# Between two layers: tile 1's last residual update and some weight splits set behind tile 0's first products, and buffers of their own for what meets there

## The chip, the cores and the metric

The kernel runs on one core of a Trainium2 chip. Its engines are named as in the profile: PE multiplies matrices, DVE and ACT do elementwise work, POOL and SP stand beside them, and SP issues the loads. Each engine has its own queue of instructions and runs it in order; semaphores let one wait for another. The metric is the device time of one execution in microseconds, as the median of several runs.

## The reference

A decoder trunk of two layers on 256 tokens of width 2048, batch 1, all in float32. Layer 0 mixes tokens with RWKV-7, layer 1 with latent attention (MLA) on a key and value store that is computed once from the residual stream. Each layer ends in a squared-ReLU MLP of width 8192. Every sub-layer is normed on both sides and gated:

```python
h = rms_norm(x, norm_g[l, 0]) * (1.0 + scale_m) + shift_m
y = rwkv7_time_mix(h, ...)  # layer 0;  mla_attention(h, ...) in layer 1
x = x + gate_m * rms_norm(y, norm_g[l, 1])
h = rms_norm(x, norm_g[l, 2]) * (1.0 + scale_f) + shift_f
y = squared_relu_mlp(h, mlp_up[l], mlp_down[l])
x = x + gate_f * rms_norm(y, norm_g[l, 3])
# between the layers, from the x that layer 0 leaves:
hs = rms_norm(x, kv_in_g)
ckr = hs @ kv_down
```

`scale_*`, `shift_*` and `gate_*` come from one conditioning vector `c` by `silu(c) @ ada_w[l] + ada_b[l]`.

## The kernel before

The 256 tokens are two token tiles of 128 (`t` is 0 or 1). The residual stream `xr` stays on the chip, tokens on partitions, 2048 values a row. Products need channels on partitions, so at the start of a sub-layer the normed residual is turned by PE and scaled (`affine4`).

Weights come from memory in units of 128x2048 float32, 1 MB, loaded by SP into a buffer `raw`. A unit is split in two halves of 128x1024 (`unit`, `hilo`): ACT casts the half to the high part `whi` (L172) and DVE subtracts to get the low part `wlo` (L173). Each product is then three matmuls (`mm3`: high x high, low x high, high x low; L218 to L220). The pool `split` holds `WB_MLP` or `WB_MLA` pairs of such halves. Where that pool is not to be used, `unit` is given other room (`spare`, `spare_part`), and the halves are then named `spare`.

The change is about three seams, where one sub-layer's last products have to become the next one's input:

1. RWKV's output projection (`proj_tail`, products `po`) to the MLP of layer 0 (`begin`, products `pup`)
2. the down products of that MLP (`pd`) to the shared latent (`kvd`, products `pl`)
3. the attention's output projection (`po`) to the MLP of layer 1 (`pup`)

At each seam the class `Residual` finishes the old sub-layer. `block(t, n, ...)` takes a block of 512 columns: it adds what lies there already, squares it on ACT for the norm (`square_sum`, written to `junk`) and multiplies it with the gate row `G`. `update(t)` takes the norm factor `rs` of tile `t` (`rstd`, a reduction `rrv` and seven small DVE steps, L151 to L168) and adds the two halves of 1024 columns to `xr` (L976), ACT squares the result for the next norm. `last` does the last block and `update` for tile 0 and for tile 1 and returns the next norm's factors `rx0` and `rx1` together.

The new sub-layer then scales the identity with tile `t`'s factor (`dg`, L1114 or L1327), and PE multiplies `xr` by it in 16 transposes a tile (`trt`, L1030), four to a group `g`. `affine4` brings a group to the input: four steps `hc`, taken in turn by DVE and ACT, a cast on ACT and a subtraction on DVE (to `h`, or `o1h` and `o1l` in seam 2). `products(t, g)` are 12 matmuls, four rows of channels times three. The order on PE is written out by hand (`manual_schedule`): 16 transposes of tile 0, (0,0), (0,1), 16 transposes of tile 1, (1,0), (1,1), (0,2), (0,3), (1,2), (1,3). On the other engines a scheduler sets the order when the program is built; `issue_after(x)` holds what is written under it back until `x` has been issued. Units 0 and 1 of the new weight go to the split pool, and units 2 and 3 to spare room, issued after tile 1's `dg`.

Of the kernel before, what the change touches and what calls it, by code (L numbers as in the profile page):

```python
# [12 lines left out]
F32 = mybir.dt.float32  # L13
F32R = mybir.dt.float32r
# [62 lines left out]
def trunk_kernel(ctx: ExitStack, tc: tile.TileContext, a, out, dbg=None):  # L77
# [93 lines left out]
    def hilo(hi, lo, x):  # L171
        ACT.copy(hi, x)  # L172
        return DVE.tensor_sub(lo, x, hi.bitcast(F32))  # L173

# [213 lines left out]
    with ExitStack() as s0:  # L388
# [3 lines left out]
        p1 = pool(s0, "p1", 1)  # L392

        XS = []
        xs0 = p1.tile([P, 4, 4, T], F32R, tag="xs0", name="xs")
# [4 lines left out]
        with ExitStack() as s1:  # L400
# [10 lines left out]
            def spot():  # L411
# [60 lines left out]
            for cb in range(4):  # L472
# [9 lines left out]
                XS.append(p1.tile([P, 4, 4, T], F32R, tag=f"xs{cb}", name="xs") if cb else xs0)  # L482
# [68 lines left out]
        with ExitStack() as s2:  # L551
# [361 lines left out]
            while nxt < KT or flying:  # L913
                if nxt < KT and len(flying) < LONG and steps >= STAGGER * nxt:
# [29 lines left out]
        with ExitStack() as s3:  # L944
# [5 lines left out]
            G0 = p1.tile([P, KT, T], F32R, tag="xs3", name="G0").bitcast(F32).rearrange("p k c -> p (k c)")  # L950
# [3 lines left out]
            class Residual:  # L954
# [16 lines left out]
                def update(self, t, then=None):  # L971
                    rs = rstd(self.ss, t, D, "rn")
# [60 lines left out]
    def affine4(t, g, ps, sc, bi, hi, lo, tp):  # L1033

        q, ks = slice(t * P, (t + 1) * P), slice(g * 4, g * 4 + 4)
        h = tp.tile([P, 4, P], F32, tag="hc", name="hc", bufs=2)
# [9 lines left out]
        hilo(hi[:, ks, q], lo[:, ks, q], h)  # L1046

    def to_channels(xn, sc, bi, hi, lo, tp, tags=("rw",), kts=range(KT)):

        for kt in kts:  # L1050
# [4 lines left out]
            h = tp.tile([P, 2, T], F32, tag="hc", name="hc", bufs=2)[:, 0, :]  # L1055
# [14 lines left out]

    def mlp(l, x, rx, ada_rate, aside=None):
        with ExitStack() as s:
            psum(s, rw=5, pj=3)

            mh = pool(s, f"mlc{l}", 1)
            m2 = pool(s, f"mlq{l}", 2)
            mp = pool(s, f"mlp{l}", 1)
            ya = mp.tile([P, 2, D], F32, name="ya")
            split["more"] = pool(s, "more", MORE_MLP)
# [23 lines left out]
            def begin():  # L1103

                A = mod_scale(l, 4, 2)
                parts = [p_ for k in range(2) for p_ in unit(a["up0"][l, k])]
# [4 lines left out]
                def turn(t, gs):  # L1111
                    if 0 in gs:
                        dg[t] = mh.tile([P, P], F32, tag="dg", name="dg", bufs=2)
                        turned.append(DVE.tensor_scalar(dg[t], ident, rx[t], None, ALU.mult).ins)  # L1114
                    for g in gs:
                        trs[t, g] = transposes(x[:, t, :], dg[t], g)

                def products(t, g):
# [3 lines left out]
                dg, turned = {}, []  # L1122
                with tc.manual_schedule(engines={mybir.EngineType.PE}):
                    for t in range(2):
                        turn(t, range(4))
                        for g in range(4):
                            affine4(t, g, trs[t, g], A, mods[l, 3], hh, hl, mh)
                            if g < 2:
                                products(t, g)
                    with tc.issue_after(turned[1]):  # L1130
                        for k in (2, 3):
                            parts += unit(a["up0"][l, k], room=spare)
                    for t in range(2):
                        for g in (2, 3):
                            products(t, g)
                for t in range(2):
                    u = mh.tile([P, 512], F32, tag="hc", name="u0", bufs=2)
# [108 lines left out]
    with ExitStack() as s4:  # L1246
# [5 lines left out]
        ckcq = qa.tile([P, 4, 4, T], F32R, tag="ckcq", name="ckcq")  # L1252
        ckT, cqT = [ckcq[:, z] for z in range(2)], [ckcq[:, 2 + z] for z in range(2)]
        qs = pool(s4, "qs", 1)
        qv = pool(s4, "qv", 1)
        q2 = pool(s4, "q2", 1)
# [20 lines left out]
        if True:  # L1277
# [4 lines left out]
            def latent(pss, gname, dst):  # L1282
# [6 lines left out]
                for j in range(4):  # L1289
# [3 lines left out]
                    h = q2.tile([P, 2, T], F32, tag="hc", name="hc", bufs=2)[:, 0, :]  # L1293
# [27 lines left out]
            parts = [p_ for k in range(2) for p_ in unit(a["kvd"][k])]  # L1321
            trs, dg, turned = {}, {}, []

            def turn(t, gs):
                if 0 in gs:
                    dg[t] = q2.tile([P, P], F32, tag="dg", name="dg", bufs=2)
                    turned.append(DVE.tensor_scalar(dg[t], ident, rx[t], None, ALU.mult).ins)  # L1327
                for g in gs:
# [243 lines left out]
```

## Time and profile before

| | us |
|---|---|
| runs | 2584.51, 2598.10, 2595.97 |
| median | 2595.97 |
| profiled execution | 2599.04 |
| its span | 2597.3 |
| PE busy in the span | 2487.8 |
| DVE busy | 1945.7 |
| ACT busy | 1312.5 |

The times inside the profile are counted from the start of the span, which is 1.7 us shorter than the time of that execution. In rows of the order in time, the columns are start, duration, engine, line, operation, what it writes and reads, the shapes and how many were merged; in square brackets stands how long the engine had been idle before it, and who ended the wait. A matmul row's duration overlaps the next one's, so distances between starts tell how fast products follow. The granted clock was 0.98 of full speed over the span.

### The profile page before, as it was taken

To read this page: it belongs to the slowest core of one execution; us is meant where nothing else is said; L and a number is where in the kernel's file an instruction comes from. 1 tells how busy PE (TensorE), PEld (TensorE's weight loads), DVE (VectorE), ACT (ScalarE), POOL (GpSimd) and SP (SyncE) were. 2 spreads that over 40 slices of the span, in tenths; PEclk is the share of its full clock that TensorE was granted. 3 is DMA by queue.
4 is the path that set the end of the run, shared out by engine and by line. 5 is a ranking of instruction groups with operands and counts; after the bars stand their busy time and mean duration, and the time that the engine had idled before them with its cause. 6 is when DMAs were issued, how large, how long until landed. Compare 5 with 4: busy or idle time off the path is not lost.

```text
span 2597.3 us, 39264 instructions
## 1 busy us (share of the span) xinstructions
PE 2487.8 (96%) x15048; PEld 2060.5 (79%) x15048; DVE 1945.7 (75%) x3823; ACT 1312.5 (51%) x2361; POOL 70.9 (3%) x150
## 2 busy tenths in 40 slices
PE   6998999999997999999999999999899999999998
PEld 3667887888776888888888878778788888888886
DVE  4787887888877788888888867776676665555555
ACT  3555675766646444444444456544544444444443
POOL 0000110111100000000000000000000000000000
PEclk8899998999998999999999999999999999999999
DMA  9755544455575688888888824657567555555553
GB/s 374 293 192 196 178 173 153 166 180 186 171 265 205 227 331 327 331 322 328 327 332 332 328 103 156 217 176 254 210 223 260 186 190 195 189 185 194 192 184 127
DMA packets 87885, 594.54 MB, mean 229 GB/s; under 512 B 10128, under 2 KB 14480, under 8 KB 16784
## 3 DMA queue, kind: packets, MB, share of 16 engines
q1 hardware_dynamic: 87696, 592.03, 63.0%
q8 instruction: 118, 1.93, 0.3%
q14 instruction: 71, 0.58, 0.1%
HBM read 589.89 MB, written 2.10 MB: 228 GB/s over the span
## 4 chain that ended last, share of the span: by engine, by line
PE 77%; DVE 8%; ACT 4%; issue 1%; DMA 1%; POOL 0%; DVEq 0%; ACTq 0%
PE pup L233 17%; PE pd L218 9%; PE pd L220 9%; PE pd L219 9%; PE pup L234 9%; DVE wlo L173 2%; DVE raw L320 1%; PE po L219 1%; PE po L220 1%; PE po L218 1%; PE rk L223 1%; PE rk L224 1%; PE rk L225 1%; PE pl L218 1%; PE ar L720 1%
## 5 line engine op out<-in xcount | busy, mean ns | idle before, releaser
L172 ACT CAST whi<-raw 128x1024 fp32r<-128x1024 f32 x729 | 743.9, 1023 | 895.1 <-PE pd L220 355.9
L173 DVE TENSOR_TENSOR wlo<-raw,whi 128x1024 fp32r<-128x1024 f32 x729 | 864.0, 1188 | 439.0 <-ACT whi L172 436.1
L233 PE MATMUL pup<-h,whi 128*128 128x512 f32 x1920 | 677.8, 398 | 0.0
L234 PE MATMUL pup<-h,wlo 128*128 128x256 f32 x1920 | 539.2, 281 | 0.0
L233 PEld LDWEIGHTS pup<-h,whi 128*128 128x128 f32 x1920 | 360.6, 188 | 88.5
L218 PE MATMUL pd<-whi,uh 128*128 128x512 f32 x1024 | 399.0, 390 | 0.0
L220 PE MATMUL pd<-whi,ul 128*128 128x512 f32 x1024 | 398.6, 389 | 0.0
L320 DVE SCALAR_TENSOR_TENSOR raw<-raw,crow 128x1024 f32<-128x1024 f32 x320 | 389.4, 1225 | 12.0 <-DMA raw<-in_adat_dram 12.0
L219 PE MATMUL pd<-wlo,uh 128*128 128x512 f32 x1024 | 398.4, 389 | 0.0
L234 PEld LDWEIGHTS pup<-h,wlo 128*128 128x128 f32 x1920 | 362.7, 189 | 0.5
L220 PEld LDWEIGHTS pd<-whi,ul 128*128 128x128 f32 x1024 | 192.2, 188 | 40.4
L218 PEld LDWEIGHTS pd<-whi,uh 128*128 128x128 f32 x1024 | 192.2, 188 | 40.0
L219 PEld LDWEIGHTS pd<-wlo,uh 128*128 128x128 f32 x1024 | 192.2, 188 | 39.5
L223 PE MATMUL rk<-xs,whi 128*128 128x256 f32 x512 | 155.5, 304 | 2.9 <-ACT rS L595 2.2
L225 PE MATMUL rk<-xs,wlo 128*128 128x256 f32 x512 | 150.1, 293 | 2.1 <-DVE wlo L173 2.0
L224 PE MATMUL rk<-xs,whi 128*128 128x256 f32 x512 | 148.6, 290 | 0.0
L223 PEld LDWEIGHTS rk<-xs,whi 128*128 128x128 f32 x512 | 98.7, 193 | 9.3 <-ACT rS L595 4.1
L225 PEld LDWEIGHTS rk<-xs,wlo 128*128 128x128 f32 x512 | 98.8, 193 | 4.5 <-DVE wlo L173 3.0
L224 PEld LDWEIGHTS rk<-xs,whi 128*128 128x128 f32 x512 | 98.7, 193 | 1.8
L732 DVE TENSOR_TENSOR xt<-ar,X 128x60 f32<-128x60 f32 (+14 forms) x240 | 49.3, 206 | 22.3 <-ACT ar L721 20.0
L1188 DVE TENSOR_TENSOR ya<-pd,ya 128x512 f32<-128x512 f32 x96 | 61.5, 682 | 0.0
L219 PE MATMUL pv<-wlo,xsv 128*128 128x512 f32 x128 | 55.1, 431 | 5.0 <-DVE wlo L173 4.8
(431 smaller groups left out, 3620.5 us busy)
## 6 DMA issues: line engine op xcount, KB each, us to landing
raw<-in_adat_dram SPq DMA_DIRECT2D x160, 1024.0 KB, 6.9
raw<-in_up_dram SPq DMA_DIRECT2D x128, 1024.0 KB, 4.9
raw<-in_dn_dram SPq DMA_DIRECT2D x128, 1024.0 KB, 4.9
early<-in_ada_dram SPq DMA_DIRECT2D x17, 1024.0 KB, 11.9
raw<-in_wr_dram SPq DMA_DIRECT2D x16, 1024.0 KB, 5.0
raw<-in_wk_dram SPq DMA_DIRECT2D x16, 1024.0 KB, 5.9
raw<-in_wo_dram SPq DMA_DIRECT2D x16, 1024.0 KB, 5.2
raw<-in_mo_dram SPq DMA_DIRECT2D x16, 1024.0 KB, 5.3
```

What stands on the lines that cost most here:

```text
L172: ACT.copy(hi, x)
L173: return DVE.tensor_sub(lo, x, hi.bitcast(F32))
L218: PE.matmul(ps, lh, rh, start=start, stop=False)
L219: PE.matmul(ps, lh, rl, start=False, stop=False)
L220: PE.matmul(ps, ll, rh, start=False, stop=stop)
L223: PE.matmul(ps, wh, xh, start=start, stop=False)
L224: PE.matmul(ps, wh, xl, start=False, stop=False)
L225: PE.matmul(ps, wl, xh, start=False, stop=stop)
L233: PE.matmul(ps, hi[:, s], x2[:, kt].rearrange("p e t -> p (e t)"), start=(kt == 0), stop=False)
L234: PE.matmul(ps[:, T:], lo[:, s], x2[:, kt, 0, :], start=False, stop=(kt == KT - 1))
L320: DVE.scalar_tensor_tensor(raw[:, s], raw[:, s], 1.0, crow[:, s], ALU.mult, ALU.mult, accum_out=part[:, kt, half : half + 1])
L1188: DVE.tensor_add(y, pss[t], y)
```

## The change

`last` now returns tile 0's factor and a function `later`, which does tile 1's update and its factor when it is called. Both seams' code goes through one new function, `tiles_first`. It splits five halves of the new weight (units 0 and 1 and the first half of unit 2) into the split pool, which holds five pairs now, and turns tile 0. After affine (0,1) it issues the second half of unit 2 into spare room, `later` and affine (0,2). The products of (0,2) come before tile 1's transposes. The split of unit 3 and affine (0,3) are issued after affine (1,1). In the attention layer the scalings `xn` of the residual come after affine (1,3).

Buffers: `hc` and `dg` move to a pool `seam` that lives through the whole program. The four blocks `xs` of the RWKV layer become four pools. `ckcq` gets a pool of its own, the pool `more` of raw units is opened ahead of the MLP's `ya`, `EARLY` goes from 3 to 4, and the build gives the scratch room of dynamic loads 8192 bytes.

```diff
-WB_MLP = 4
-WB_MLA = 4
+WB_MLP = 5
+WB_MLA = 5
...
-EARLY = 3
+EARLY = 4
...
+    def split_part(raw, at, room=None):
+        if room:
+            hi, lo = room()
+        else:
+            hi = split["hi"].tile([P, 1024], F32R, tag="whi", name="whi")
+            lo = split["lo"].tile([P, 1024], F32R, tag="wlo", name="wlo")
+        hilo(hi, lo, raw[:, at * 1024 : at * 1024 + 1024])
+        return hi, lo
...
+    seam = pool(ctx, "seam", 1)
...
                     self.block(0, n, pss[0], more)
                     self.update(0)
+                    rs0 = rstd(self.xs, 0, D, "rx0")
                     self.block(1, n, pss[1], more)
-                    rs = [rstd(self.xs, 0, D, "rx0")]
-                    self.update(1)
-                    rs.append(rstd(self.xs, 1, D, "rx1"))
-                    return rs
+                    rs1 = rstd(self.ss, 1, D, "rn")
+
+                    def later():
+                        self.update(1, rs=rs1)
+                        return rstd(self.xs, 1, D, "rx1")
+
+                    return rs0, later
...
+    def tiles_first(rx, units, room, turn, affine, products):
+        rs0, later = rx
+        parts = [p_ for src in units[:2] for p_ in unit(src)]
+        raw = load(units[2])
+        parts.append(split_part(raw, 0))
+
+        def wait(*ins):
+            for i_ in ins:
+                held.enter_context(tc.issue_after(i_))
+
+        with tc.manual_schedule(engines={mybir.EngineType.PE}):
+            turn(0, rs0)
+            for g in range(2):
+                ready = affine(0, g)
+                products(parts, 0, g)
+            with ExitStack() as held:
+                wait(*ready)
+                parts.append(split_part(raw, 1, room))
+                rs1 = later()
+                affine(0, 2)
+            products(parts, 0, 2)
+            turn(1, rs1)
+            for g in range(2):
+                ready = affine(1, g)
+                products(parts, 1, g)
+            with ExitStack() as held:
+                wait(*ready)
+                parts.extend(unit(units[3], room=room))
+                affine(0, 3)
+            products(parts, 0, 3)
+            for g in (2, 3):
+                ready = affine(1, g)
+                products(parts, 1, g)
+        return ready
...
-            for t in range(2):
-                for n in range(2):
-                    s = slice(n * 1024, (n + 1) * 1024)
-                    DVE.tensor_scalar(xn[:, t, s], x[:, t, s], rx[t], None, ALU.mult)
+            ready = tiles_first(rx, [a["kvd"][k] for k in range(4)], spare_part, turn, affine, products)
+            with tc.issue_after(ready[1]):
                 for t in range(2):
+                    for n in range(2):
+                        s = slice(n * 1024, (n + 1) * 1024)
+                        DVE.tensor_scalar(xn[:, t, s], x[:, t, s], rxs[t], None, ALU.mult)
...
-    nc = bacc.Bacc("TRN2", target_bir_lowering=False, num_devices=1)
+    nc = bacc.Bacc("TRN2", target_bir_lowering=False, num_devices=1, dynamic_dma_scratch_size=8192)
```

What this does to the order on the engines is seen at three places. The number after L is the line of the kernel that is listed, so L976 and L989, or L1327 and L1370, are the same statement before and after.

On DVE at seam 2, from update(0) (`xr`) to tile 0's `dg`, before the change (`ya` is the MLP's sum, `rrv` to `rsu` are steps of the norm):

```order
L976 SCALAR_TENSOR_TENSOR xr<-ya,rsy,xr 128x1024 x2
L967 TENSOR_TENSOR ya<-pd_15940,ya 128x512
L376 TENSOR_REDUCE rrv<-ssx 128x1
L151 TENSOR_SCALAR rsy<-rrv 128x1
L157 SCALAR_TENSOR_TENSOR rst<-rsy,rrv 128x1
L163 SCALAR_TENSOR_TENSOR rsy<-rst,rsy 128x1
L157 SCALAR_TENSOR_TENSOR rst<-rsy,rrv 128x1
L166 TENSOR_SCALAR rsu<-rst 128x1
L167 TENSOR_TENSOR rsu<-rsu,rst 128x1
L168 SCALAR_TENSOR_TENSOR rsy<-rsu,rsy 128x1
L1327 TENSOR_SCALAR dg<-ident,rsy 128x128
```

After the change, the last twelve rows of the same stretch:

```order
L166 TENSOR_SCALAR rsu<-rst 128x1
L982 TENSOR_TENSOR ya<-ya,G 128x512
L167 TENSOR_TENSOR rsu<-rsu,rst 128x1
L389 TENSOR_REDUCE rrv<-ss 128x1
L173 TENSOR_TENSOR wlo<-raw,whi 128x1024
L168 SCALAR_TENSOR_TENSOR rsy<-rsu,rsy 128x1
L151 TENSOR_SCALAR rsy<-rrv 128x1
L173 TENSOR_TENSOR wlo<-raw,whi 128x1024
L157 SCALAR_TENSOR_TENSOR rst<-rsy,rrv 128x1
L173 TENSOR_TENSOR wlo<-raw,whi 128x1024
L163 SCALAR_TENSOR_TENSOR rsy<-rst,rsy 128x1
L1370 TENSOR_SCALAR dg<-ident,rsy 128x128
```

Two more rows `wlo` stand between these and update(0): all five halves are now split there, where none was, and steps of tile 1's norm have come in among them.

On ACT at the same place, the squares of the old blocks and of `xr`, and the casts among them, before the change:

```order
L386 ACTIVATE junk,ss<-ya 128x512 x3
L386 ACTIVATE junk,ssx<-xr 128x1024
L172 CAST spare<-raw 128x1024
L386 ACTIVATE junk,ssx<-xr 128x1024
L172 CAST spare<-raw 128x1024
L386 ACTIVATE junk,ss<-ya 128x512
L172 CAST spare<-raw 128x1024 x2
L386 ACTIVATE junk,ssx<-xr 128x1024 x2
L1043 ACTIVATE hc<-trt,pcol 128x128 x3
```

And after:

```order
L399 ACTIVATE junk,ss<-ya 128x512 x3
L399 ACTIVATE junk,ssx<-xr 128x1024
L172 CAST whi<-raw 128x1024
L399 ACTIVATE junk,ssx<-xr 128x1024
L172 CAST whi<-raw 128x1024
L399 ACTIVATE junk,ss<-ya 128x512
L172 CAST whi<-raw 128x1024 x3
L1061 ACTIVATE hc<-trt,pcol 128x128 x2
```

The casts of the first five halves stand where those of units 2 and 3 stood, and the squares of tile 1's `xr` have gone behind the first `hc`.

On DVE at seam 3, the end of tile 1's update and tile 0's `dg`, before the change:

```order
L167 TENSOR_TENSOR rsu<-rsu,rst 128x1
L168 SCALAR_TENSOR_TENSOR rsy<-rsu,rsy 128x1
L976 SCALAR_TENSOR_TENSOR xr<-yG_18116,rsy,xr 128x1024 x2
L1114 TENSOR_SCALAR dg<-ident,rsy 128x128
L376 TENSOR_REDUCE rrv<-ssx 128x1
```

After, from `dg` to the first step of affine (0,2):

```order
L1167 TENSOR_SCALAR dg<-ident,rsy 128x128
L166 TENSOR_SCALAR rsu<-rst 128x1
L167 TENSOR_TENSOR rsu<-rsu,rst 128x1
L168 SCALAR_TENSOR_TENSOR rsy<-rsu,rsy 128x1
L1059 TENSOR_SCALAR hc<-trt,A_18856,mod_92 128x128 x3
L1065 TENSOR_TENSOR h_18855<-hc,h_18855 128x4x128
L1059 TENSOR_SCALAR hc<-trt,A_18856,mod_92 128x128
L1065 TENSOR_TENSOR h_18855<-hc,h_18855 128x4x128
L989 SCALAR_TENSOR_TENSOR xr<-yG_18133,rsy,xr 128x1024
L173 TENSOR_TENSOR spare<-raw,spare 128x1024
L989 SCALAR_TENSOR_TENSOR xr<-yG_18133,rsy,xr 128x1024
L1059 TENSOR_SCALAR hc<-trt,A_18856,mod_92 128x128
```

Tile 1's update (`xr`) has gone from ahead of `dg` to behind affine (0,1), with half a spare split between its halves. Ahead of this `dg`, five rows `wlo` stand among the norm steps as in seam 2, and in seam 1 one `wlo` stands ahead of update(0) and the add of tile 1's block ahead of the multiply of tile 0's.

More of the change, by code (lines that the diff above doesn't have):

```diff
@@ L391, in trunk_kernel @@
         splits(s0, WB)
-        p1 = pool(s0, "p1", 1)
+        p1 = [pool(s0, f"p1{j}", 1) for j in range(4)]
         XS = []
-        xs0 = p1.tile([P, 4, 4, T], F32R, tag="xs0", name="xs")
+        xs0 = p1[0].tile([P, 4, 4, T], F32R, tag="xs0", name="xs")
         def xs_at(w, z, kt):
@@ L1045, in affine4, with to_channels @@
                 ACT.activation(h[:, j, :], ps[:, o], AF.Identity, scale=s, bias=b)
-        hilo(hi[:, ks, q], lo[:, ks, q], h)
-    def to_channels(xn, sc, bi, hi, lo, tp, tags=("rw",), kts=range(KT)):
+        cast = ACT.copy(hi[:, ks, q], h).ins
+        return cast, DVE.tensor_sub(lo[:, ks, q], h, hi[:, ks, q].bitcast(F32)).ins
+    def to_channels(xn, sc, bi, hi, lo, tags=("rw",), kts=range(KT)):
         for kt in kts:
@@ L1109, in begin, with turn, affine, products @@
                 trs = {}
[L1111 to L1118, printed above, removed]
+                def turn(t, rs):
+                    dg = seam.tile([P, P], F32, tag="dg", name="dg", bufs=2)
+                    DVE.tensor_scalar(dg, ident, rs, None, ALU.mult)
+                    for g in range(4):
+                        trs[t, g] = transposes(x[:, t, :], dg, g)
+                def affine(t, g):
+                    return affine4(t, g, trs[t, g], A, mods[l, 3], hh, hl)
+                def products(parts, t, g):
                     for kt in range(4 * g, 4 * g + 4):
                         part_products(pss[t], t, kt, (*parts[kt // 2], kt % 2), hh, hl, kt == 0, kt == KT - 1)
-                dg, turned = {}, []
-                with tc.manual_schedule(engines={mybir.EngineType.PE}):
-                    for t in range(2):
[L1125 to L1135, printed above, removed]
+                tiles_first(rx, [a["up0"][l, k] for k in range(4)], spare, turn, affine, products)
                 for t in range(2):
-                    u = mh.tile([P, 512], F32, tag="hc", name="u0", bufs=2)
+                    u = seam.tile([P, 512], F32, tag="hc", name="u0", bufs=2)
                     ACT.activation(u, pss[t], AF.Relu)
@@ L1319, in spare_part @@
                 return spares.pop(0)
[L1321 to L1328, printed above, removed]
-                    trs[t, g] = transposes(x[:, t, :], dg[t], g, ("rw", "sc", "po")[g % 3])
@@ L1331, in products, with turn, affine @@
-            def products(t, g):
+            trs, rxs = {}, []
+            def turn(t, rs):
+                rxs.append(rs)
+                dg = seam.tile([P, P], F32, tag="dg", name="dg", bufs=2)
+                DVE.tensor_scalar(dg, ident, rs, None, ALU.mult)
+                for g in range(4):
+                    trs[t, g] = transposes(x[:, t, :], dg, g, ("rw", "sc", "po", ("rw", "sc")[t])[g])
+            def affine(t, g):
+                return affine4(t, g, trs[t, g], cols("kv_in_g", 0, KT), None, hsh, hsl)
@@ L1354, in trunk_kernel @@
             A1 = mod_scale(1, 1, 0)
[L1355 removed]
+            to_channels(xn, A1, mods[1, 0], hh, hl, ("rw", "po"))
             latent(pc, "kv_norm", ckT)
```

50 lines of the change are left out of this document (18 added, 32 removed).

## The prediction

> **What bounds the kernel.** I read the page's busy line first, then its chain, then the busy table by stages, then the order in time of PE, DVE and ACT at the three places where PE stops.
>
> ```profile
> PE 2487.8 (96%) x15048; PEld 2060.5 (79%) x15048; DVE 1945.7 (75%) x3823; ACT 1312.5 (51%) x2361; POOL 70.9 (3%) x150
> PE 77%; DVE 8%; ACT 4%; issue 1%; DMA 1%; POOL 0%; DVEq 0%; ACTq 0%
> 809.00:853.00 44.00, 32.59 (x164) 27.27 (x163) 32.39 (x74) 24.86 (x46) 0.20 (x2) 0.88 0.54 200
> 853.00:1500.00 647.00, 647.00 (x3290) 548.98 (x3288) 556.28 (x799) 292.49 (x369) 0.00 (x0) 1.00 0.85 319
> 1545.00:1588.00 43.00, 36.38 (x173) 30.36 (x172) 33.10 (x79) 25.18 (x49) 0.74 (x2) 0.88 0.30 100
> 1853.00:1895.00 42.00, 33.65 (x166) 28.43 (x165) 27.56 (x62) 24.50 (x44) 0.00 (x0) 0.88 0.49 179
> 1895.00:2500.00 605.00, 605.00 (x3102) 514.83 (x3100) 379.40 (x485) 269.93 (x349) 0.00 (x0) 1.00 0.58 201
> ```
>
> The columns after the length of the stage are the busy time of PE, its weight loads, DVE, ACT and POOL, then the clock granted. PE carries 77% of the chain. In both MLP stretches it is busy for the whole 647 and 605 us, so a deeper pool of weight halves, another order of loads or a moved scaling is worth nothing there. In the three seams PE is idle for 11.4, 6.6 and 8.4 us, 26 us in all. The kernel is the same up to the first seam, so the change is decided in those 26 us.
>
> Seam 1 (`po` to `pup`), seam 2 (`pd` to `pl`), seam 3 (`po` to `pup`), PE only:
>
> ```profile
> 809.45 0.39 PE L220 MATMUL po<-whi,ol 128*128 128x512 f32 x1
> 818.57 5.56 PE L1030 MATMUL trt<-dg,xr 128*128 128x128 f32 x32 [8.74 <-DVE dg L1114]
> 826.07 0.50 PE L218 MATMUL pup<-whi,h 128*128 128x512 f32 x1 [1.94 <-ACT h L172]
> 827.34 0.50 PE L220 MATMUL pup<-whi,h 128*128 128x512 f32 x1 [0.53 <-DVE h L173]
> 852.90 0.40 PE L220 MATMUL pup<-spare,h 128*128 128x512 f32 x1
> ...
> 1550.57 6.45 PE L1030 MATMUL trt<-dg,xr 128*128 128x128 f32 x32 [4.95 <-DVE dg L1327]
> 1558.69 0.50 PE L218 MATMUL pl<-whi,o1h 128*128 128x512 f32 x1 [1.67 <-ACT o1h L172]
> 1559.97 0.63 PE L218 MATMUL pl<-whi,o1h 128*128 128x512 f32 x1
> 1569.76 0.38 PE L1054 MATMUL trx<-ident,xn 128*128 128x128 f32 x2
> 1587.13 0.40 PE L220 MATMUL pl<-spare,o1l 128*128 128x512 f32 x1
> ...
> 1860.88 6.59 PE L1030 MATMUL trt<-dg,xr 128*128 128x128 f32 x32 [7.11 <-DVE dg L1114]
> 1869.06 0.50 PE L220 MATMUL pup<-whi,h 128*128 128x512 f32 x1 [1.03 <-DVE h L173]
> 1874.18 3.73 PE L1030 MATMUL trt<-dg,xr 128*128 128x128 f32 x32
> 1878.85 0.50 PE L220 MATMUL pup<-whi,h 128*128 128x512 f32 x1
> 1894.62 0.40 PE L220 MATMUL pup<-spare,h 128*128 128x512 f32 x1
> ```
>
> Each seam has one long wait, for `dg` (the identity scaled by tile 0's norm factor), then the 16 transposes, then a shorter wait for the first affine. Two numbers decide: when `dg` comes, and how long PE needs from `dg` to the last product. Those spans are now 34.9 us (818.24, quoted below, to 853.1), 37.1 us (1550.23 to 1587.4) and 34.3 us (1860.55 to 1894.9).
>
> **When dg comes.** DVE runs its rows in order, so what the new order sets ahead of `dg` moves it:
>
> ```profile
> 808.48 1.21 DVE L173 TENSOR_TENSOR wlo<-raw,whi 128x1024 fp32r<-128x1024 f32 x1
> 809.61 0.68 DVE L969 TENSOR_TENSOR yo<-yo,G 128x512 f32<-128x512 f32 x1
> 818.24 0.28 DVE L1114 TENSOR_SCALAR dg<-ident,rsy 128x128 f32<-128x128 f32 x1
> 1548.56 0.16 DVE L376 TENSOR_REDUCE rrv<-ssx 128x1 f32<-128x3 f32 x1 [1.46 <-ACT junk L386]
> 1550.23 0.29 DVE L1327 TENSOR_SCALAR dg<-ident,rsy 128x128 f32<-128x128 f32 x1
> 1855.05 0.16 DVE L376 TENSOR_REDUCE rrv<-ssx 128x1 f32<-128x3 f32 x1 [1.34 <-ACT junk L386]
> 1857.00 0.15 DVE L168 SCALAR_TENSOR_TENSOR rsy<-rsu,rsy 128x1 f32<-128x1 f32 x1
> 1858.15 2.48 DVE L976 SCALAR_TENSOR_TENSOR xr<-yG,rsy,xr 128x1024 f32<-128x1024 f32 x2
> 1860.55 0.28 DVE L1114 TENSOR_SCALAR dg<-ident,rsy 128x128 f32<-128x128 f32 x1
> ...
> 1859.53 1.06 ACT L386 ACTIVATE junk<-xr 128x1024 bf16<-128x1024 f32 x1 [3.86 <-DVE xr L976]
> 1480.87 1.05 ACT L172 CAST whi<-raw 128x1024 fp32r<-128x1024 f32 x1 [0.33 <-DMA raw<-in_kvd_dram]
> 1481.95 3.71 DVE L173 TENSOR_TENSOR wlo<-raw,whi 128x1024 fp32r<-128x1024 f32 x3 [0.15 <-ACT whi L172]
> 1840.37 4.63 DVE L173 TENSOR_TENSOR wlo<-raw,whi 128x1024 fp32r<-128x1024 f32 x4 [0.97 <-ACT whi L172]
> ```
>
> A `wlo` occupies DVE for 1.14 us of pitch (4.63 us for four in a row; 808.48 to 809.61). The last three rows matter most: today most halves of the first units of seams 2 and 3 are split long before the seam, at 1481 and 1840, under the products of the stage before. In the new order they stand behind update(0), in the chain of norm steps that ends in `dg`.
>
> - Seam 1: one more `wlo` (unit 2's first half) stands ahead of update(0), and the add of tile 1, which must wait for the last product (809.45 + 0.39 = 809.84), now comes ahead of the multiply that began at 809.61: 1.14 + 0.37 = **+1.5 us**. Nothing else moves; update(1) stood behind `dg` already.
> - Seam 2: five `wlo`. The first fits into the idle 1.46 us ahead of `rrv`, for +0.1. Four follow: 4.56. The multiply of tile 1 with `G` now comes ahead of `dg` too (0.60 of pitch, by the 0.68 row), with some steps of tile 1's chain (0.4). The small steps wait less for each other with work between: -0.3. **+5.4 us**, bounds 4.6 (only the four `wlo`) and 5.8 (without that relief).
> - Seam 3: five `wlo`, 5.7, less update(1), 2.4, which stood ahead of `dg` although its result is not used there; less about 0.6, for steps of tile 1's chain (most of those between 1857.15 and 1858.15) that now come behind `dg` or overlap: **+2.7 us**, bounds 2.5 and 3.3. Without the splits this seam would gain 3.4: tile 0's factor is there at 1857.15, and `dg` starts at 1860.55.
>
> Sum for `dg`: **+9.6 us**. Other queues: POOL's rows are the same; SP issues the same loads, the third unit's where it stood and the fourth's past two or more others, but its products come last of all. ACT's casts take the places of the `spare` casts in seam 2 and in seam 3 run in ACT's idle 3.86 us ahead of the squares (the 1859.53 row).
>
> **From dg to the last product.**
>
> ```profile
> 1558.66 0.69 DVE L173 TENSOR_TENSOR o1l<-hc,o1h 128x512 fp32r<-128x512 f32 x1
> 1866.63 0.62 ACT L172 CAST h<-hc 128x512 fp32r<-128x512 f32 x1
> 1875.27 0.46 ACT L1045 ACTIVATE hc<-trt,mod,A 128x128 f32<-128x128 f32 x1 [1.70 <-PE trt L1030]
> 1875.76 0.41 DVE L1041 TENSOR_SCALAR hc<-trt,A,mod 128x128 f32<-128x128 f32 x1 [1.38 <-ACT hc L1045]
> ```
>
> Gain: update(1), two squares and spare splits no longer stand between the transposes and the first affines. Four `hc` steps alternate at 0.41 and 0.46, 1.7 us a group; with cast and subtraction a group is done 3.0 us after its transposes, and these take 1.6 us a group. So (0,0) and (0,1) are ready when the 16th transpose ends, and the waits of 1.94 + 0.53, 1.67 and 1.03 go.
>
> What is late next: group (0,2). Behind (0,1)'s subtraction (about 7.1 us after `dg`) DVE has two halves of update(1) and a spare subtraction (2.4 + 1.14, to 10.7), ACT then the second square (1.06 and its read, to 11.9), and only then come the last `hc`, the cast and the subtraction (13.3, 14.0). PE ends (0,0), (0,1) at 0.33 + 6.4 + 24 x 0.227 = 12.2 (1878.85 to 1894.62 is 70 products in 15.8, so 0.227 each). So a new wait S of 1.4 to 2.6 us stands ahead of (0,2); I take 2.0, and 2.6 in seam 1, where the transposes took 0.9 less. The affines (0,3), (1,2), (1,3) stand behind the split of the fourth unit, two subtractions and two casts: a wait Q of 0 to 2.3 us; I take 1.0, 2.0 and 1.2.
>
> With all 96 products (21.8), the second transposes (3.7, which hide the affine (1,0)) and 0.5 of starts (0.33 from `dg` to the first transpose), the span is 26.0 + transposes (5.5, 6.4, 6.4) + S + Q:
>
> - seam 1: 26.0 + 5.5 + 2.6 + 1.0 = 35.1, against 34.9: +0.2
> - seam 2: 26.0 + 6.4 + 2.0 + 2.0 = 36.4, against 37.1 less 0.7 for `trx` pairs (the 1569.76 row, and one more) that now come later: 0
> - seam 3: 26.0 + 6.4 + 2.0 + 1.2 = 35.6, against 34.3: +1.3
>
> Sum +1.5 us; with S and Q at their bounds -5 to +5.
>
> **Clock.** A short wait can cost more than itself:
>
> ```profile
> 1559.50:1562.50 3.00, 3.00 (x7) 2.38 (x8) 2.96 (x7) 1.61 (x5) 0.00 (x0) 0.50 0.03 8
> ```
>
> After the 1.67 us wait ahead of 1558.69 the granted clock is 0.50 and products start every 0.43 us (the 0.63 us row) for 3.4 us, which loses 1.7 us. The waits of 1.94 and 1.03 us in the other seams had no such stretch. One wait in three did it, and its loss stands in seam 2's 37.1 and so is taken off above. With three new waits of about 2 us I count one such stretch after the change: **+1.7 us**, bounds 0 and 5.
>
> The Trainium skill, page "TensorE: Matmul & The Clock Gate", section "HAM oscillation — how this bites in real kernels", says that the clock falls after idle gaps of more than about 3.4 us. By that rule no wait here would cost a half clock and the sum would be 1.7 us lower. The 1559.5 row disagrees, since the gap ahead was 1.67 us, so the term stays.
>
> **Sum.** 9.6 + 1.5 + 1.7 = +12.8 us. Elsewhere nothing is on the path: the moved `xn` scalings hit only the start of the `trx` transposes (1.5 us at most), and the order of the attention's heads may give or take 2. The profiled execution took 2599.04 us, 3.1 above the median 2595.97 of the runs shown. The delays are the same on either: 2595.97 + 12.8 = **2608.8**; I say 2608.5.
>
> **Rivals.**
> 1. The splits are covered and the change does what its rows allow: `dg` does not move in seams 1 and 2, comes 3.4 us sooner in seam 3, and the waits of 1.94 + 0.53, 1.67 with its half clock 1.7, and 1.03 go. That is 10.3 us less some 1 us of new waits, about 2587. It needs the `wlo` of seams 2 and 3 to run in DVE's gaps. Against it: the only gap ahead of `dg` is the 1.46 us (1.34 in seam 3), room for one of five. It decides from four hidden `wlo` per seam on. Chance 0.06.
> 2. The new waits S and Q are small (1.4 and 0) and the clock holds: +9.6 - 5 = +5, about 2601. For it: ACT has slack in these seams (25 of 43 us busy). Chance 0.38 for this and all else between 2594 and 2605.
> 3. Every seam is slowed again behind S: +9.6 + 1.5 + 3 x 1.7 = +16, and S at 2.6 adds 1: 2612 to 2615. For it the 1559.97 row; against it the 1.94 wait without such a stretch. Chance 0.18.
> 4. The likeliest, +9 to +15, chance 0.38. In 0.15 of these the clock holds through every new wait: 9.6 + 1.5, 2607.1.
>
> **How the numbers follow.** Half a per cent, 13 us, is about what a measurement of this kernel can tell from no change. Its upper bound, 2609, lies at my forecast, so same and slower share nearly all: half of the likeliest and all of rival 3 lie above, with some room for run differences: slower 0.42, same 0.51, faster 0.07. The range from 2593 to 2615 leaves out rival 1 and the ends of the bounds.
>
> **What would show it.** In the changed profile PE's wait for `dg` is 10.2, 10.4 and 9.8 us (8.74, 4.95 and 7.11 now), with the `wlo` rows of L173 between update(0) and `dg`. The first `pup` and `pl` products follow the transposes without a wait; a wait of about 2 us for the cast of `h` or `o1h` stands 24 products later. The MLP stretches stay at full PE. The forecast is wrong if that wait in seam 2 is under 7 us (then casts and subtractions overlap more than a pitch of 1.14 allows), or if S is near 0.

## The result, and the profile after

The changed kernel takes 2605.3 us (median of 11 runs, 2600.4 to 2615.9) against 2592.9 (11 runs, 2582.7 to 2604.7) for the kernel before, taken in turn on the same chip. The ratio is 1.0052, with a 95% interval of 1.0033 to 1.0071. By the ratio that is 13.5 us slower, with 8.6 to 18.4 as the interval's ends. The forecast was 12.5 us slower. The profiled execution took 2608.07 us, its span is 2606.3 us, and the mean clock is 0.981.

First the profile page's busy line of the changed kernel, and then its table by stages (length, busy time of PE, PEld, DVE, ACT and POOL, granted clock, DMA share, GB/s). The first, third and fourth rows are the three seams, the other two are the MLP stretches.

```profile
PE 2482.7 (95%) x15048; PEld 2056.3 (79%) x15048; DVE 1947.2 (75%) x3823; ACT 1313.2 (50%) x2361; POOL 69.8 (3%) x150
799.00:846.00 47.00, 34.15 (x162) 28.32 (x161) 31.99 (x74) 25.62 (x47) 0.20 (x2) 0.82 0.46 169
846.00:1500.00 654.00, 654.00 (x3326) 554.90 (x3325) 556.04 (x798) 291.17 (x370) 0.00 (x0) 1.00 0.85 316
1539.00:1590.00 51.00, 36.49 (x171) 29.51 (x169) 37.16 (x81) 28.48 (x52) 0.20 (x2) 0.83 0.36 125
1855.50:1902.00 46.50, 33.62 (x164) 27.88 (x163) 31.67 (x66) 29.02 (x49) 0.00 (x0) 0.85 0.51 190
1902.00:2500.00 598.00, 598.00 (x3056) 507.94 (x3056) 374.52 (x478) 265.55 (x342) 0.00 (x0) 1.00 0.58 202
```

All engines do the same work as before, and PE is still never idle in the two MLP stretches. The seams hold the difference. PE is idle in them for 12.9, 14.5 and 12.9 us, 40 us in all instead of 26, and the clock there is 0.82 to 0.85 instead of 0.88. PE in order of time, seams 1, 2 and 3:

```profile
809.83 6.46 PE L1048 MATMUL trt<-dg,xr 128*128 128x128 f32 x32 [10.14 <-DVE dg L1167]
816.05 0.48 PE L228 MATMUL pup<-whi,h 128*128 128x512 f32 x1
824.27 0.50 PE L228 MATMUL pup<-whi,h 128*128 128x512 f32 x1 [2.50 <-ACT h L1064]
825.96 0.63 PE L230 MATMUL pup<-whi,h 128*128 128x512 f32 x1
...
1549.61 5.26 PE L1048 MATMUL trt<-dg,xr 128*128 128x128 f32 x32 [9.99 <-DVE dg L1370]
1554.63 0.47 PE L228 MATMUL pl<-whi,o1h 128*128 128x512 f32 x1
1563.18 0.80 PE L228 MATMUL pl<-whi,o1h 128*128 128x512 f32 x1 [2.73 <-ACT o1h L1064]
1577.79 0.50 PE L228 MATMUL pl<-spare,o1h 128*128 128x512 f32 x1 [0.85 <-ACT o1h L1064]
1579.45 0.50 PE L230 MATMUL pl<-spare,o1l 128*128 128x512 f32 x1 [0.93 <-DVE o1l L1065]
...
1865.56 5.97 PE L1048 MATMUL trt<-dg,xr 128*128 128x128 f32 x32 [9.69 <-DVE rsu L166]
1880.00 0.56 PE L228 MATMUL pup<-whi,h 128*128 128x512 f32 x1 [2.98 <-ACT h L1064]
```

The wait for `dg` is 10.14, 9.99 and 9.69 us, against 8.74, 4.95 and 7.11. (In seam 3 the wait is put down to a step beside it; `dg` itself starts at 1865.22.) The first products follow the transposes at once. A wait stands 24 products later, ahead of group (0,2): 2.50, 2.73 and 2.98 us. Behind each of those three waits, and once more behind the two waits at the end of seam 2, the granted clock is halved. The windows of the same profile (a fourth like them begins at 1880.3):

```profile
826.00:829.00 3.00, 3.00 (x9) 2.32 (x8) 0.00 (x0) 0.00 (x0) 0.00 (x0) 0.50 1.02 429
1563.50:1566.00 2.50, 2.50 (x7) 1.88 (x7) 0.55 (x2) 0.00 (x0) 0.00 (x0) 0.50 0.02 7
1580.50:1583.00 2.50, 2.50 (x7) 1.97 (x6) 2.29 (x4) 0.37 (x1) 0.00 (x0) 0.50 0.88 364
```

Each of these stretches lasts 3.41 us by the clock's own record, and with PE busy all through it loses half of that, 1.7 us. DVE in order of time in seam 2 shows why `dg` is late, with the five `wlo` between update(0) and `dg`:

```profile
1538.01 2.48 DVE L989 SCALAR_TENSOR_TENSOR xr<-ya,rsy,xr 128x1024 f32<-128x1024 f32 x2
1541.51 1.23 DVE L173 TENSOR_TENSOR wlo<-raw,whi 128x1024 fp32r<-128x1024 f32 x1 [0.41 <-ACT whi L172]
...
1543.61 1.22 DVE L173 TENSOR_TENSOR wlo<-raw,whi 128x1024 fp32r<-128x1024 f32 x1
...
1545.54 1.22 DVE L173 TENSOR_TENSOR wlo<-raw,whi 128x1024 fp32r<-128x1024 f32 x1
...
1546.81 1.22 DVE L173 TENSOR_TENSOR wlo<-raw,whi 128x1024 fp32r<-128x1024 f32 x1
...
1548.07 1.22 DVE L173 TENSOR_TENSOR wlo<-raw,whi 128x1024 fp32r<-128x1024 f32 x1
1549.27 0.28 DVE L1370 TENSOR_SCALAR dg<-ident,rsy 128x128 f32<-128x128 f32 x1
```

To compare seams between runs I use one measure: the time from the last product of the old sub-layer to the 1000th matmul after it, less the same time in the first profile of the kernel before. The changed kernel loses 4.14, 8.47 and 6.94 us by it, 19.6 in all, and nearly nothing outside the seams from there on. Yet its profiled execution reached the first seam 10.1 us earlier than the profiled one before (799.3 against 809.4), though the order of the work up to there is the same. The first 430 us, of before and then of after:

```profile
0.00:430.00 430.00, 380.24 (x2835) 293.42 (x2835) 321.94 (x865) 238.48 (x544) 28.76 (x81) 0.93 0.61 225
```

```profile
0.00:430.00 430.00, 379.44 (x2950) 293.00 (x2951) 329.34 (x892) 246.07 (x565) 30.23 (x84) 0.96 0.63 231
```

The clock was 0.93 in one and 0.96 in the other, and in the same time the second had done 115 more matmuls. This part varies from execution to execution of one program, as the runs below show, so a profile's whole length says less here than its seams.

### The profile page after: what moved, and what is told of

Its sections match the earlier page's. It is cut to its first block, busy times and chain, and to the rows that moved or that the text cites. A ratio compares the mean times of both kernels' runs of the same rounds, so it can differ in the third digit from the quotient of the medians.

```text
span 2606.3 us, 39189 instructions
## 1 busy us (share of the span) xinstructions
PE 2482.7 (95%) x15048; PEld 2056.3 (79%) x15048; DVE 1947.2 (75%) x3823; ACT 1313.2 (50%) x2361; POOL 69.8 (3%) x150
## 4 chain that ended last, share of the span: by engine, by line
PE 82%; DVE 10%; ACT 4%; DMA 2%; issue 2%; SPq 0%; POOL 0%; DVEq 0%; ACTq 0%
PE pup L243 17%; PE pd L228 9%; PE pd L230 9%; PE pd L229 9%; PE pup L244 9%; DVE wlo L173 2%; PE po L229 1%; PE rk L233 1%; PE po L230 1%; PE po L228 1%; PE rk L234 1%; PE rk L235 1%; PE pv L229 1%; PE pv L230 1%; PE pv L228 1%
## 5 line engine op out<-in xcount | busy, mean ns | idle before, releaser
L243 PE MATMUL pup<-h,whi 128*128 128x512 f32 x1920 | 679.1, 399 | 0.0
L244 PE MATMUL pup<-h,wlo 128*128 128x256 f32 x1920 | 539.4, 281 | 0.0
L243 PEld LDWEIGHTS pup<-h,whi 128*128 128x128 f32 x1920 | 360.8, 188 | 89.7
L244 PEld LDWEIGHTS pup<-h,wlo 128*128 128x128 f32 x1920 | 362.7, 189 | 0.8
L745 DVE TENSOR_TENSOR xt<-ar,X 128x60 f32<-128x60 f32 (+14 forms) x240 | 48.9, 204 | 21.2 <-ACT ar L734 18.8
```

The costliest lines, as they stand in the source:

```text
L243: PE.matmul(ps, hi[:, s], x2[:, kt].rearrange("p e t -> p (e t)"), start=(kt == 0), stop=False)
L244: PE.matmul(ps[:, T:], lo[:, s], x2[:, kt, 0, :], start=False, stop=(kt == KT - 1))
```

## The experiments

The theory ahead of them is the prediction's: the seams lose by splits that now stand ahead of `dg`, by the wait S ahead of (0,2), and by the half clock behind S. Each experiment takes away or moves one of these, or several together. In the table "seams" are seams 1, 2 and 3 by the measure above; ratios are against the kernel before on the same chip.

| run | ratio [95%] | seams, us | sum |
|---|---|---|---|
| changed kernel | 1.0052 [1.0033, 1.0071] | +4.14, +8.47, +6.94 | +19.6 |
| changed kernel again | one execution | +2.99, +7.93, +7.14 | +18.1 |
| four pairs | 1.0017 [1.0006, 1.0029] | +3.55, +3.11, -0.31 | +6.4 |
| affine (0,2) first | 1.0023 [1.0007, 1.0039] | -0.37, +2.28, +2.63 | +4.5 |
| fillers | 1.0038 [1.0025, 1.0050] | +0.93, +7.00, +5.19 | +13.1 |
| kernel before, fillers | 1.0006 [0.9994, 1.0019] | -1.2, -0.7, 0.0 | -1.9 |
| kernel before again | one execution | +0.01, -1.52, +0.03 | -1.5 |
| kernel before, a third | one execution | -0.03, +0.06, +1.23 | +1.3 |
| splits apart | 0.9990 [0.9975, 1.0004] | +0.53, -0.42, -1.13 | -1.0 |
| fifth split behind `dg` | 0.9991 [0.9977, 1.0005] | +0.79, -0.51, -3.41 | -3.1 |
| the same with fillers | 0.9976 [0.9960, 0.9992] | -1.99, -1.99, -5.03 | -9.0 |
| both halves behind `dg` | 0.9963 [0.9946, 0.9979] | -2.25, -1.69, -4.18 | -8.1 |

**Four pairs: the splits alone.** Why do the splits of seams 2 and 3 stand behind update(0) at all, when before they were done at 1481 and 1840? The addresses in the built program answer it. With five pairs in both pools, the latent attention's pool lies at bytes 150112 to 191072 of each partition and the MLP's pool begins at 186336. The two share 4736 bytes, and one half of unit 0 lies on a half that the old sub-layer's last products still read. With four pairs in either pool nothing is shared, and in the built order the splits of both seams stand ahead of them again. The edit:

```diff
-WB_MLP = 5
-WB_MLA = 5
+WB_MLP = 4
+WB_MLA = 4
...
-        parts.append(split_part(raw, 0))
+        parts.append(split_part(raw, 0, room))
```

> The changed kernel with four pairs of weight halves in the split pool again; the first half of unit 2 goes to spare room. In the order the splits of units 0 and 1 then stand under the products of the stage before in seams 2 and 3, as before the change. Theory A (splits ahead of dg cost 9 us): PE's waits for dg fall from 10.1, 10.0, 9.7 to about 10.1, 5.1 and 3.7 us, the rest of each seam stays, and the kernel is about 11 us faster than the changed one, within 3 us of the kernel before. Theory B (the new order of PE and the late update(1) cost the time, DVE and ACT have the same work to do in a seam wherever it stands): dg comes sooner but the wait ahead of (0,2) grows by as much, and the time stays within 3 us of the changed kernel's.

PE in order of time, the three transposes of tile 0 and one wait S, then the splits on ACT and DVE:

```profile
816.41 6.60 PE L1048 MATMUL trt<-dg,xr 128*128 128x128 f32 x32 [9.77 <-DVE dg L1167]
830.84 0.50 PE L228 MATMUL pup<-spare,h 128*128 128x512 f32 x1 [2.35 <-ACT h L1064]
1551.48 6.02 PE L1048 MATMUL trt<-dg,xr 128*128 128x128 f32 x32 [5.51 <-DVE dg L1370]
1861.08 6.50 PE L1048 MATMUL trt<-dg,xr 128*128 128x128 f32 x32 [3.74 <-DVE dg L1167]
```

```profile
1481.43 3.13 ACT L172 CAST whi<-raw 128x1024 fp32r<-128x1024 f32 x3 [0.54 <-DMA raw<-in_kvd_dram]
1844.00 4.63 DVE L173 TENSOR_TENSOR wlo<-raw,whi 128x1024 fp32r<-128x1024 f32 x4 [1.05 <-ACT whi L172]
```

The splits are back at 1481 and 1844. The waits for `dg` in seams 2 and 3 fall from 9.99 and 9.69 to 5.51 and 3.74 us; seam 3's is 3.4 below that of the kernel before, which is what the prediction worked out for that seam without its splits. S stays (2.35, 1.98 and 2.39 us), each with a half-clock stretch behind it. S did not grow, as by the second expectation it should have. Against 18.8 us, the mean of the two profiles of the changed kernel, the seams give back 12.5 us, and by the ratios it is 9 (0.0035 of 2593). So the late splits are shown to cost about that much. The kernel is still 4.4 us slower than the one before by the ratio, where at most 3 was expected.

**Affine (0,2) first: S alone.**

```diff
                 parts.append(split_part(raw, 1, room))
-                rs1 = later()
                 affine(0, 2)
+                rs1 = later()
```

> The changed kernel with affine (0,2) written ahead of tile 1's update. Theory A (the wait ahead of (0,2) is update(1), its squares and a split in front of the affine): that wait falls from 2.5, 2.7, 3.0 to under 1 us, tile 1's dg comes later and PE waits for it up to 1.5 us a seam, and 3 to 6 us are gained over the changed kernel, the half-clock stretches behind (0,2) included. Theory B (the wait only moves from (0,2) to tile 1's transposes): within 2 us of the changed kernel, and as many half-clock stretches.

PE in order of time at tile 1's transposes in seam 1, then the windows of seams 1 and 2 where half clock stood before:

```profile
835.20 3.84 PE L1048 MATMUL trt<-dg,xr 128*128 128x128 f32 x32 [1.09 <-DVE dg L1167]
```

```profile
826.00:836.00 10.00, 8.91 (x43) 7.16 (x42) 7.22 (x16) 5.12 (x9) 0.10 (x1) 1.00 0.65 246
1560.00:1575.00 15.00, 15.00 (x82) 12.08 (x81) 9.82 (x24) 8.95 (x17) 0.10 (x1) 1.00 0.21 72
```

S is gone, the waits for `dg` are the changed kernel's (10.15, 10.00 and 9.69), tile 1's `dg` is waited for by 1.09, 0 and 1.39 us instead, and the clock holds at 1.00 behind these shorter waits. By rows that is 8.2 - 2.5 = 5.7 us of waiting and 5.1 to 6.8 of half clock. The seams gain 14.3, the ratios 7.5 (0.0029). Both are more than the 3 to 6 expected, although that had the half clock in it. The gains of the two runs must not be added up as shares of the loss: by the seams they come to 26.8 us, more than the 18.8 that are lost.

**Fillers: the clock alone.** In this and the other runs with fillers, PE multiplies the identity by itself while it waits for tile 0's `dg`; nothing reads the result. These matmuls are extra work.

```diff
+    WARM = [34, 34, 33]
...
+            warm = rbank("warm")
+            for i in range(WARM.pop(0)):
+                PE.matmul(warm[:, :P], ident, ident, start=True, stop=True)
             turn(0, rs0)
```

> The changed kernel with 34, 34 and 33 matmuls of the identity with itself, 0.23 us each, written to a bank that nobody reads, on PE while it waits for tile 0's dg in the three seams. Theory A (the clock that falls in these waits costs its time): the transposes take 3.7 us instead of 6.5, 5.3 and 6.0, and the kernel is 5 to 8 us faster than the changed one. Theory B (the affines are then the bound): the first products wait 1 to 2 us for the affine, the wait ahead of (0,2) grows by the rest, and the gain is under 3 us.

```profile
816.39 3.81 PE L1048 MATMUL trt<-dg,xr 128*128 128x128 f32 x32 [2.60 <-issue]
829.01 0.72 PE L228 MATMUL pup<-whi,h 128*128 128x512 f32 x1 [2.60 <-ACT h L1064]
1552.91 5.38 PE L1048 MATMUL trt<-dg,xr 128*128 128x128 f32 x32 [2.41 <-DVE dg L1375]
```

The transposes take 3.81, 5.38 and 3.84 us instead of 6.46, 5.26 and 5.97. In seam 2 the clock was halved again behind a gap of 2.41 us after the last filler; behind gaps of 2.60 and 2.33 us in seams 1 and 3 it was not. S (2.60, 1.99 and 2.55 us) and the stretches behind it stay. The gain is 5.7 us by the seams and 3.6 by the ratios, between the two expectations (5 to 8, and under 3), so the time does not decide between them. The waits that the second expectation named did not come: the first products wait 0.21 us at most, and S did not grow.

**The kernel before with fillers** (30, 13 and 23 at the same place):

> The kernel before with 30, 13 and 23 such matmuls in PE's waits for tile 0's dg. Theory A (before the change the first affine stands behind update(1) and its squares, so PE waits for it whenever the transposes end): the transposes take 3.7 us, the wait for the first affine grows by nearly as much, 0 to 3 us are gained. Theory B (the clock alone costs the time): 7 us are gained.

```profile
1553.87 3.84 PE L1030 MATMUL trt<-dg,xr 128*128 128x128 f32 x32 [2.04 <-DVE dg L1332]
1560.90 0.80 PE L218 MATMUL pl<-whi,o1h 128*128 128x512 f32 x1 [3.19 <-ACT o1h L172]
```

The transposes of seam 2 are 2.6 us shorter, and the wait for the first affine behind them grows from 1.67 to 3.19 us: there the affine chain on DVE and ACT is the bound, and faster transposes mostly wait longer. In seams 1 and 3 the gaps behind the fillers, 2.11 and 1.95 us, were followed by half clock again (transposes of 5.38 and 5.47 us), so only seam 2 shows this cleanly. The ratio holds 1. In the changed kernel the first products follow the transposes without a wait, so fillers gained there.

**The changed kernel once more:**

> The changed kernel once more, to see how much of its profile repeats. If seam times belong to the order, PE's waits are again 10.1, 10.0, 9.7 and 2.5, 2.7, 3.0 us within 0.2, and the seams lose 17 to 20 us against the kernel before. What differs from run to run lies ahead of 430 us. If the clock's stretches of half speed fall where chance puts them, some of the four behind short waits are missing, and the seams lose 1.7 us less for each.

It took 2611.9 us. The waits for `dg` repeat within 0.01 us (10.14, 10.00 and 9.69), and the same four half-clock stretches stand at the same places. S is 2.68, 2.36 and 2.35, so it repeats less well than the 0.2 us expected. Part of what differs arises behind a seam: the 200th matmul behind seam 1 comes 4.09 us late in the first profile and 4.13 in this one, the 1000th 4.14 and 2.99. Two more executions of the kernel before:

> The kernel before once more, for its seams. Against its first profile the changed kernel's seams lose 18 to 19 us in two profiles, while the timed difference is 12 to 13. If the first profile of the kernel before had short seams by chance, this one's are 3 to 6 us longer, by half-clock stretches behind its waits of 1.94, 1.67 and 1.03 us or slower transposes. If they repeat within 1 us, the rest of the difference lies ahead of the first seam, where both kernels have the same order.

> As the run before: a third profile of the kernel before, same expectations.

They took 2589.7 and 2595.5 us, with seams within 1.5 us of the first profile, so the 18 to 20 us that the changed kernel loses in its seams are far outside what its seams vary by. The time of the first seam is not so steady. It came at 809.4, 814.0 (with fillers), 801.6 and 804.7 us in four executions that share the first 800 us of the kernel before, and at 797.8 to 809.0 in nine of the changed kernel and its variants. It follows the half-clock time ahead of that seam: 78.5 us of it with 814.0, 64.9 with 809.4, 41.0 with 799.3, 37.5 with 797.8. All thirteen profiles lie within 2.1 us of one line, 0.38 us later for each us of half clock.

**Splits apart.** Both remedies: four pairs in the latent attention's pool so that the pools share no bytes, five in the MLP's, in seam 2 the fifth half in spare room, and affine (0,2) ahead of `later`.

```diff
-WB_MLA = 5
+WB_MLA = 4
...
+    FIFTH = [0, 1, 0]
...
-        parts.append(split_part(raw, 0))
+        parts.append(split_part(raw, 0, FIFTH.pop(0) and room))
...
-                rs1 = later()
                 affine(0, 2)
+                rs1 = later()
```

> The changed kernel with affine (0,2) ahead of update(1), and four pairs in the attention layer's split pool alone, so that its bytes no longer overlap those of the MLP's five pairs; its fifth half goes to spare room. In the order the splits of seams 2 and 3 then stand ahead of the seam. Theory A (two separate causes, splits ahead of dg and update(1) ahead of the affine): waits for dg of 10.1, 5.1 to 5.5 and 3.7 us, no wait ahead of (0,2), no half-clock stretch behind it, seams shorter than the kernel before's by about 0.4, 2.6 and 3.3 us: 4 to 8 us faster than the kernel before. Theory B (whatever comes sooner waits for the affines or tile 1's factor): the two gains do not add, and the time is that of the kernel before within 3 us.

```profile
828.36 5.47 PE L1048 MATMUL trt<-dg,xr 128*128 128x128 f32 x32 [1.86 <-DVE dg L1169]
1851.66 6.20 PE L1048 MATMUL trt<-dg,xr 128*128 128x128 f32 x32 [4.77 <-DVE dg L1169]
```

2590.6 against 2592.5 us: the loss is gone, so the two causes together account for all of it. The gain of 6.3 us in the seams that the first expectation had is only 1.0, and the time is what the second one said. Two rows say why. In seam 3 `dg` is waited for by 4.77 us, not the 3.74 of the four pairs, since the fifth split still stands ahead of it. In seam 1 tile 1's `dg` came 1.86 us late and the clock fell behind that wait, so that the transposes took 5.47 us.

**Fifth split behind `dg`.** The fifth half is issued after tile 0's `dg`, which `turn` returns for it:

```diff
-        parts.append(split_part(raw, 0, FIFTH.pop(0) and room))
...
-            turn(0, rs0)
+            with tc.issue_after(turn(0, rs0)):
+                parts.append(split_part(raw, 0, FIFTH.pop(0) and room))
```

> As the run before, and the fifth half is split behind tile 0's dg, under the transposes. Theory A: the wait for dg in seam 1 falls by the 1.14 us of that split, to about 9.0, nothing else moves: 5 to 9 us faster than the kernel before. Theory B (the split then delays the first affine): the first products wait 1 us in each seam, and the time is that of the run before or longer.

```profile
1852.90 6.21 PE L1048 MATMUL trt<-dg,xr 128*128 128x128 f32 x32 [3.74 <-DVE dg L1169]
```

One split less ahead of `dg` is worth 1.0 us of wait in seams 1 and 3 (10.14 to 9.13, 4.77 to 3.74), close to the pitch of 1.14 us. The 1.89 us wait in seam 1 and its half clock stay. By the ratio this is no different from the run before it, and the 5 to 9 us expected against the kernel before did not come.

**The same with fillers** (36, 18 and 12):

> As the run before, and 36, 18 and 12 matmuls of the identity on PE in the waits for tile 0's dg, written to a bank that nobody reads. Theory A (with the affines off the path the clock is the last loss in a seam): transposes of 3.8 us instead of 5.7 to 6.4, 3 to 6 us faster than the run before. Theory B (the affines of (0,1) and (0,2) bound the products after the transposes): the products wait as much longer, and the gain is under 2 us.

PE in order of time, the transposes of tile 0 in seams 1 and 2 and those of tile 1 between them, and the windows of the three seams:

```profile
807.40 3.81 PE L1048 MATMUL trt<-dg,xr 128*128 128x128 f32 x32 [1.15 <-issue]
821.31 3.81 PE L1048 MATMUL trt<-dg,xr 128*128 128x128 f32 x32 [1.15 <-issue]
1537.42 3.84 PE L1048 MATMUL trt<-dg,xr 128*128 128x128 f32 x32 [1.40 <-DVE dg L1377]
```

```profile
798.00:840.00 42.00, 39.28 (x240) 33.78 (x240) 33.13 (x76) 25.95 (x47) 0.21 (x2) 1.00 0.54 199
1531.50:1575.00 43.50, 39.78 (x224) 32.24 (x222) 35.88 (x90) 27.02 (x54) 0.20 (x2) 1.00 0.28 97
1838.00:1880.00 42.00, 39.25 (x221) 32.74 (x220) 29.80 (x65) 26.95 (x48) 0.00 (x0) 1.00 0.48 177
```

With gaps of at most 1.40 us the clock is 1.00 throughout all three seams, and every set of transposes takes 3.8 us. The seams gain 5.9 us over the run before, the ratios 3.9 (0.0015). 2586.4 us against 2592.5: this version is 6 us faster than the kernel before, and with that faster than the changed one.

**Both halves behind `dg`.** As the last, with the second half of unit 2 issued there too, ahead of the first affines:

```diff
+            with tc.issue_after(turn(0, rs0)):
+                parts.append(split_part(raw, 0, FIFTH.pop(0) and room))
+                parts.append(split_part(raw, 1, room))
...
-                parts.append(split_part(raw, 1, room))
                 affine(0, 2)
```

> The run apart_warm with both halves of unit 2 split behind tile 0's dg, so that none stands between affine (0,1) and (0,2). Theory A (tile 1's factor is the last wait of a seam, and that split stands ahead of it): the wait for tile 1's dg falls from 1.15, 0 and 1.20 us to 0.2 or less, 1 to 3 us faster than apart_warm, which took 2586.4 beside 2592.5 of the kernel before. Theory B (with transposes of 3.8 us the first affine is due so early that 2.3 us of splits on DVE ahead of it show): the first products wait 1 to 2 us in each seam, and it is 0 to 4 us slower than apart_warm.

```profile
815.07 0.50 PE L228 MATMUL pup<-whi,h 128*128 128x512 f32 x1 [1.32 <-ACT h L1064]
```

The wait for tile 1's `dg` is gone, and in its place the first products wait 1.32, 1.39 and 1.29 us: the split on ACT and DVE costs at least as much there (4.0 us of waiting in the three seams, where the run before had 2.8 at the two places together). 2583.8 us against 2595.4, the fastest that was run; whether it is faster than the one before it isn't resolved, as the two intervals overlap.

## Why the prediction came out as it did

- **`dg` later: right.** +1.40, +5.04 and +2.58 us by PE's waits, 9.0 in all, where the prediction summed 1.5, 5.4 and 2.7. Four pairs took away 10.4 us of those waits in seams 2 and 3, where four splits a seam went back ahead of update(0), and moving a single split was worth 1.0. What the prediction did not see is the reason, which is 4736 shared bytes and not the order in which the code is written: with the pools apart the same code has the splits early.
- **First products and S: right.** No wait behind the transposes; S at 2.50, 2.73 and 2.98 us where 2.6, 2.0 and 2.0 were taken. In seam 1, DVE does `later`'s update and the spare split ahead of the square, and ACT's cast comes last:

```profile
817.27 1.28 DVE L989 SCALAR_TENSOR_TENSOR xr<-yo,rsy,xr 128x1024 f32<-128x1024 f32 x1
...
819.60 1.28 DVE L989 SCALAR_TENSOR_TENSOR xr<-yo,rsy,xr 128x1024 f32<-128x1024 f32 x1
820.97 1.06 ACT L399 ACTIVATE junk<-xr 128x1024 bf16<-128x1024 f32 x1 [1.24 <-DVE xr L989]
823.60 0.62 ACT L1064 CAST h<-hc 128x512 fp32r<-128x512 f32 x1
```

- **Clock: the term that was mis-sized.** One stretch was counted after the change, +1.7 us with 0 to 5 as bounds; the one that the kernel before has was taken off in the span of seam 2. Four came, 6.8 us, past the upper bound. The step that failed is "One wait in three did it", taken over from three waits of 1.0 to 1.9 us to new ones of 2.5 to 3.0; the fourth stretch came behind Q. The mechanism of rival 3 (half clock behind every S) is what happened, at 1.7 us a stretch as it had it, and its chance of 0.18 was too low; its total of 2612 to 2615 is above the timed 2605.3. The 0.15 for a clock that holds through every new wait was spent on something that no run with the waits S showed. The Trainium skill, page "TensorE: Matmul & The Clock Gate", section "HAM oscillation — how this bites in real kernels", puts the limit at idle gaps above about 3.4 us; these waits were all below 3.0, and the measurement decides. The same page's section "What's actually happening" gives the gate a window of 3413 ns that runs free; the stretches of 3.41 us agree with that length.
- **From `dg` to the last product, without the clock:** 18.8 us (the mean of 19.6 and 18.1) less 9.0 and 6.8 leaves 3.0, where 1.5 was summed. The waits came nearly as summed: between `dg` and the last product PE is idle for 10.4 and 9.6 us in the two profiles of the changed kernel and for 5.6 in the first of the kernel before, where 10.8 (S and Q) and 5.2 were taken. S is longer than taken (8.2 against 6.6), and Q is there in seam 2 alone, 0.85 + 0.93; in seams 1 and 3 PE has other products of the MLP between (L243 and L244, from 839.93 on in seam 1). But the sum has a slip. It sets built-up spans of 26.0 + transposes + S + Q against measured ones. The same build-up with the kernel before's own waits (and 0.7 for `trx` and 1.7 of half clock in seam 2) gives 34.0, 36.5 and 33.4 us, where 34.9, 37.1 and 34.3 were measured, so 2.4 us were left out of the difference. The prediction's own waits, less the old stretch, are 10.8 - 5.2 - 1.7 = +3.9 and not +1.5.
- **The sum: in part luck.** The seams lose 18.8 us in two profiles against 12.8 forecast: 5.1 more by the clock, 1.5 more by the span, 0.6 less by `dg`. The timed difference is 13.5 with 18.4 as its upper end. So the forecast time was met with some help from what happens outside the seams, and this part is open. One explanation would be that the changed program always runs its first 800 us faster, by its addresses. Then the timed difference would lie below the seams' sum by the same amount in all eight versions of it. It lies 5.3, 1.9, 3.2, 1.6 and 1.5 us below in five (changed, four pairs, fillers, splits apart, both halves behind) and 1.5, 0.8 and 2.8 above in the other three, 1 below in the mean. That speaks against a fixed gain of some 5 us, and is within what the first 800 us vary by. The buffers that moved and `EARLY` stay as they are in all eight versions, and none of those without the two causes is slower than the kernel before.
- **Rivals 1 and 2** did not happen: `wlo` found no gap ahead of `dg`, and S was not small. The cover that rival 1 needed exists, though: with the pools apart four splits a seam are done ahead of it, and together with affine (0,2) first that took the whole loss away.

## What to carry to other kernels

When a seam waits for one small instruction, list everything that its engine's queue puts ahead of it: here five splits of 1.14 us stood ahead of a 0.28 us `dg` in two seams, and the reason was two pools of different stages that shared 4736 bytes, which no line of the code says. Count the clock with a wait: here each of the eleven PE waits of 2.35 to 3.19 us ahead of products cost 1.7 us of half clock on top of itself, and no single wait of 1.40 us or less did. Fillers kept the clock in all six seams where the gap behind the last one was 1.40 us or less, and in three of six where it was 1.95 to 2.60. In seam 2 of the kernel before they gained little, because there the products wait for the elementwise chain behind PE and not for PE.

## What the chip showed that was not expected

- A half-clock stretch of 3.41 us followed all twelve waits S that were seen, in the changed kernel's two profiles, with four pairs and with fillers (1.98 to 2.98 us). One also followed waits of 1.89, 1.86, 1.67 and 1.63 us. None followed waits of 2.03, 1.94, 1.92 and 1.75 us in the kernel before and of 2.07 in it with fillers, nor those of 1.06 to 1.40 us in the later versions. The pair of 0.85 and 0.93 us at the end of seam 2 was followed by one in the changed kernel's two profiles and with fillers, and by none in the six other versions that have it. So between 1.6 and 2.1 us the length of the wait alone does not decide.
- In each of the thirteen profiles every change of the granted clock lies on one grid of 3413.33 ns, within 5 ns over the whole span. Where a wait falls on that grid differs from execution to execution, and this may be what decides; no run here shows that it does.
- With the same order of work, executions reach the first seam with a spread of 16 us (797.8 to 814.0), and that spread goes with the half-clock time ahead of it (37.5 to 78.5 us). It is larger than the effect of this change.
